# The sums T1 and T3 of a weight pair by an accumulating transfer, T2 and T4 on GpSimd one form earlier

## The chip, the cores and the metric

The kernel runs on one core of a Trainium2 chip. The metric is the device time of one execution, in microseconds; of several executions the median is compared. Five engines work side by side, each on its own list of instructions: TensorE (PE, with its weight loads PEld), VectorE (DVE), ScalarE (ACT), GpSimd (POOL) and SyncE (SP), which here only issues DMA transfers. Instructions wait for one another through semaphores.

## The reference

One layer of an encoder trunk on x of 512 positions by 1024 channels, in float32:

```python
h = _rmsnorm(x, g_pre_mix)
proj = h @ w_in                       # 1024 x 7168: q, k, v, g, u, sv, a_ret, a_sgu
...
y_ret = _retention_branch(q, k, v, g, ret_decay_logit, w_ret_o)
y_sgu = _sgu_branch(u, sv, sgu_ln_g, sgu_ln_b, w_spatial, b_spatial, w_sgu_o)
merged = jax.nn.sigmoid(a_ret) * y_ret + jax.nn.sigmoid(a_sgu) * y_sgu
x = x + _rmsnorm(merged @ w_out, g_post_mix)
h2 = _rmsnorm(x, g_pre_ffn)
x = x + _rmsnorm(_conv_gated_mlp(h2, w_up, conv_w, conv_b, w_down), g_post_ffn)
```

`w_up` is 1024 x 5632, `w_down` 2816 x 1024. The change concerns how the weights of `u`, of the two gates `a_ret` and `a_sgu`, and of most of `w_up` are brought in.

## The kernel before, in words

**Precision.** Each float32 operand is split into a high part (a copy to float32r on ACT, line 79) and a low part (source minus high part on DVE, line 86); `split` does both. A product is three matmuls: high by high, high by low, low by high.

**Pairs.** Two neighbouring weight blocks, each 128 x 1024 (four contraction tiles of 128 columns, two halves of S = 512), are multiplied in a Strassen-like scheme with seven products instead of eight. The weights come in seven forms: the blocks B11, B21 and B22 and the sums T1 = B11 + B12, T2 = T1 + B22, T3 = B12 + B22 and T4 = T2 + B21. Class `Pair` (line 676) multiplies them in the order B11, B21, T1, T2 (`part1`), T3 (`part2`), T4, B22 (`part3`); each product is twelve matmuls of 128x256. Between products ACT copies a result out of PSUM (`copy`, such as u<-ps, sig<-ps, c<-ps) or DVE adds it to another. There are twenty pairs:

- the U stage: four pairs, back to back, each with its `part3` behind the next one's `part1`;
- the gates: eight pairs in two halves of four (the first beside the retention's output block, the second beside the SGU's), with an ordinary block of 24 matmuls (`f_block`) after `part1` and one around `part3`;
- the couples: eight pairs of the up-projection, each with two `f_block`s as in the gates.

**Staging.** `wall` in device memory holds all weight blocks, in the order of use, arranged by the host; for pairs `_two` and `_up` lay out the blocks. A load is one 512 KB transfer issued from SP into a tile of the `raw` ring, which has four tiles (`raw_tile`, line 120); a tile is given to its next user when everything that reads it is done. Split blocks and forms go into the `w4` ring of nine slots (`slot`, line 126). `w_get` (line 203) hands out the next weight and emits the units behind it, up to nine slots ahead, so that loads, sums and splits stand in the engines' lists well ahead of the matmuls that use them. The Tile framework puts the instructions of each engine in an order and gives out buffers; SP issues all weight loads in the order of `wall`.

**A pair's forms before** (`w_form`, line 156): at the form B11 two loads bring `a` = [B11 | B12] and `b` = [B22 | B21] (lines 160 and 161). At T1 a third raw tile `t` is taken; DVE adds T1 into its first half (line 167) and T3 over B12 in `a` (line 168), and POOL adds T2 into the second half of `t` (line 169). At T4 POOL adds T4 over T2 (line 171). Each form is then split, the high part on ACT and the low part on DVE.

**Around the pairs.** POOL also issues the four xT loads ahead of the U stage (line 658, for the last two x tiles of each half, scaled by ACT on line 255) and adds the two gates' parts (line 806). Before the first pair, DVE multiplies the retention's output by its gate (L615), and PE transposes the result (L605 and L624, through `transposed` and `last_turn`).

Of the kernel before, what the change touches and what calls it, by code (L numbers as in the profile page):

```python
# [13 lines left out]
ALU = mybir.AluOpType  # L14
# [3 lines left out]
S = 512  # L18
# [29 lines left out]
def tile_block(ctx: ExitStack, tc, xT, x, wall, par, cs, wsp, bsp, gpost, gffn, out):  # L48
    nc = tc.nc
# [6 lines left out]
    def nm(s):  # L56
        uid[0] += 1
        return f"{s}_{uid[0]}"

    def blk(dt=F32, n="blk", shape=(P, S)):  # L60
        return sb.tile(list(shape), dt, tag="blk", bufs=NBLK, name=nm(n))

    def tmp(n="tmp", shape=(P, S)):
        return sb.tile(list(shape), F32, tag="tmp", bufs=6, name=nm(n))
# [19 lines left out]
    def split(hi, lo, src):  # L84
        copy(hi, src)
        nc.vector.tensor_sub(lo, src, as32(hi))  # L86
# [7 lines left out]
    i = 0  # L94
    while i < NW:
# [7 lines left out]
        elif i == UP0 + 2 * COUPLES[0][0]:  # L103
# [3 lines left out]
            i = UP0 + 2 * COUPLES[-1][1] + 2  # L107
# [10 lines left out]
    w_ready, w_pos, w_held, w_raw = {}, [0, 0], [0], {}  # L118

    def raw_tile():  # L120
        return sb.tile([P, 1024], F32, tag="raw", bufs=4, name=nm("raw"))
# [4 lines left out]
    def slot(n, at=0, w=1024):  # L126
        return sb.tile([P, 1088], F32R, tag="w4", bufs=9, name=nm(n))[:, at : at + w]
# [28 lines left out]
    def w_form(form, i):  # L156

        if form == "B11":
            a, b = raw_tile(), raw_tile()
            nc.sync.dma_start(a, wall[i])  # L160
            nc.sync.dma_start(b, wall[i + 1])
            w_raw["B11"], w_raw["B12"] = a[:, :S], a[:, S:]
            w_raw["B22"], w_raw["B21"] = b[:, :S], b[:, S:]
        elif form == "T1":
            t = raw_tile()
            w_raw["T1"], w_raw["T2"], w_raw["T3"], w_raw["T4"] = t[:, :S], t[:, S:], w_raw["B12"], t[:, S:]
            nc.vector.tensor_add(w_raw["T1"], w_raw["B11"], w_raw["B12"])  # L167
            nc.vector.tensor_add(w_raw["T3"], w_raw["B12"], w_raw["B22"])
            nc.gpsimd.tensor_tensor(out=w_raw["T2"], in0=w_raw["T1"], in1=w_raw["B22"], op=ALU.add)  # L169
        elif form == "T4":  # L170
            nc.gpsimd.tensor_tensor(out=w_raw["T4"], in0=w_raw["T2"], in1=w_raw["B21"], op=ALU.add)
        w = slot("wf", 0, 1088)
        lo, hi = w[:, AT_64 : AT_64 + S], w[:, S + AT_192 : 2 * S + AT_192]
        split(hi, lo, w_raw[form])
        return hi, lo
# [21 lines left out]
    def w_unit(u):  # L197
        return w_block(u[1]) if u[0] == "blk" else (w_down if u[0] in "qt" else w_form)(*u)
# [67 lines left out]
    for k in range(KD):  # L266
# [18 lines left out]
        for m in range(8):  # L285
            c = slice(m * P, (m + 1) * P)
# [5 lines left out]
    T0, T1 = slice(0, 256), slice(256, 512)  # L292
# [73 lines left out]
    for m in range(8):  # L366
        t = blk(n="qkraw")
# [286 lines left out]
    for n, acc in enumerate(t_group()):  # L654
        if n < 2:
            for k in (n + 2, n + 6):
                t = tmp("xT")
# [83 lines left out]
    for j in range(KD // 2):  # L741
        p = Pair(AF.Gelu_apprx_tanh, lambda: blk(n="u"), None, rbc)
# [52 lines left out]
    for j in range(KD // 2):  # L795
        for o, t in gated_pair(ogh, ogl, late if j == 0 else None):
            b = blk(n="r")
# [221 lines left out]
    i = 0  # L1019
    while i < NF:  # L1020
        if i in couples:
            p = Pair(None, lambda: tmp("c"), (h2h, h2l, h2forms))
# [179 lines left out]
def _parts(a, n, w):  # L1202

    k = a.shape[0] // P
    return a.reshape(k, P, n, w).transpose(2, 1, 0, 3).reshape(n, P, k * w)
# [15 lines left out]
def _two(a):  # L1221

    b = _parts(a, 8, P).reshape(4, 2, P, 2, S)
    return np.stack([
        np.concatenate([b[:, 0, :, 0], b[:, 1, :, 0]], -1), np.concatenate([b[:, 1, :, 1], b[:, 0, :, 1]], -1),
    ], 1)


def _up(a):

    for i, _ in COUPLES:
        b, c = a[2 * i].reshape(P, 2, S), a[2 * i + 1].reshape(P, 2, S)
        a[2 * i : 2 * i + 2] = np.stack([
            np.concatenate([b[:, 0], c[:, 0]], -1), np.concatenate([c[:, 1], b[:, 1]], -1),
        ])
    return a


def _gates(a, w):

    return np.concatenate([_two(a), _parts(w, 8, P).reshape(4, 2, P, 1024)], 1).reshape(16, P, 1024)
# [79 lines left out]
```

## Time and profile before

| | |
|---|---|
| device time, median of 3 runs | 825.94 us (825.88 to 827.58) |
| the profiled execution | 827.49 us, of which the profile's span is 825.7 us |
| granted TensorE clock | 0.999 of full speed |
| DVE additions for T1 and T3 | 40, 30.9 us together |
| POOL additions for T2 and T4 | 40, 62.9 us together |
| read from device memory | 88.19 MB |
| first pair's loads issued / last couple's T4 | 171.0 us / 657.6 us into the span |

In a row of the profile stand the start and the duration in us (or, in groups, the total busy time and the mean of one in ns), the engine, the line of the kernel, the operation, the tile written <- the tiles read, and the shape; behind an arrow in brackets stand the time the engine sat idle before it and what ended it. Rows "SPq" are transfers at the time SP issues them. L12 is line 12 of the kernel before. The windows' rows give, for a stretch of the span, the busy time and the number of instructions of PE, PEld, DVE, ACT and POOL, then the granted PE clock, the DMA engines' busy share and the GB/s that they moved.

### The profile page before, as it was taken

The numbers are of one execution on the slowest core, as the hardware profiler recorded it, in microseconds if no ns is written. First come the engines' busy times: TensorE is split into PE (matmuls) and PEld (weight loads), VectorE is DVE, ScalarE is ACT, GpSimd is POOL, SyncE is SP. The second block draws the span as 40 slices with busy tenths as digits, with TensorE's granted clock in tenths as the row PEclk, the third lists the DMA queues.
The fourth block names the chain that finished last, engine by engine and source line by source line (L and its number), as shares of the span: only waits on it lengthen the run. The fifth ranks groups of instructions, "written<-read, shape, count | busy, mean of one in ns | idle before, by whom it ended". The sixth has DMA issues, their size and how long they took to land.

```text
span 825.7 us, 13263 instructions
## 1 busy us (share of the span) xinstructions
PE 815.4 (99%) x5152; PEld 735.0 (89%) x5152; DVE 661.4 (80%) x1101; ACT 440.8 (53%) x771; POOL 101.0 (12%) x102
## 2 busy tenths in 40 slices
PE   9999999999999999999999999999999999999996
PEld 7888888888899999999988898899999998999996
DVE  7489897878797777767765568979899899988967
ACT  6636445546665444444445685556566566544531
POOL 0010000102121111132211211210111200000001
PEclk9999999999999999999999999999999999999999
DMA  8733222212223232222349111322322341233244
GB/s 294 246 116 102 77 77 77 77 52 78 90 102 129 103 102 80 101 101 103 108 166 339 48 55 55 103 102 103 102 103 102 102 154 52 77 115 129 96 147 154
DMA packets 29215, 93.24 MB, mean 113 GB/s; under 512 B 3360, under 2 KB 4000, under 8 KB 29152
## 3 DMA queue, kind: packets, MB, share of 16 engines
q1 hardware_dynamic: 26928, 86.85, 30.2%
q0 software_dynamic: 1360, 4.46, 1.6%
q10 hardware_dynamic: 864, 1.09, 0.4%
q8 instruction: 40, 0.66, 0.3%
q14 instruction: 23, 0.19, 0.1%
HBM read 88.19 MB, written 4.19 MB: 112 GB/s over the span
## 4 chain that ended last, share of the span: by engine, by line
PE 91%; DVE 6%; ACT 1%; issue 1%; DMA 0%; POOL 0%; DVEq 0%; SPq 0%; POOLq 0%; ACTq 0%
PE ps L692 23%; PE ps L217 12%; PE ps L218 12%; PE ps L219 12%; PE ps L1058 8%; PE ps L481 5%; PE ps L480 5%; PE ps L482 5%; PE ps L836 2%; PE ps L837 2%; PE ps L838 2%; PE ps L1074 1%; PE ps L761 1%; DVE fl L86 1%; PE ps L279 1%
## 5 line engine op out<-in xcount | busy, mean ns | idle before, releaser
L86 DVE TENSOR_TENSOR wl<-raw,wh 128x1024 fp32r<-128x1024 f32 (+1 forms) x93 | 109.1, 1182 | 48.9 <-PE ps L692 24.2
L79 ACT ACTIVATE wf<-raw 128x512 fp32r<-128x512 f32 x140 | 85.3, 627 | 102.7 <-PE ps L218 34.0
L86 DVE TENSOR_TENSOR wf<-raw,wf 128x512 fp32r<-128x512 f32 x140 | 111.1, 808 | 23.3 <-ACT wf L79 22.4
L692 PE MATMUL ps<-sh,wf 128*128 128x256 f32 x640 | 119.5, 277 | 0.0
L79 ACT ACTIVATE wh<-raw 128x1024 fp32r<-128x1024 f32 (+2 forms) x95 | 93.3, 993 | 37.4 <-DMA raw<-wall 17.0
L692 PEld LDWEIGHTS ps<-sh,wf 128*128 128x128 f32 x640 | 101.1, 188 | 0.8 <-ACT u L79 0.2
L217 PE MATMUL ps<-h2h,wh 128*128 128x512 f32 (+1 forms) x256 | 92.4, 363 | 0.7 <-ACT h2h L906 0.7
L218 PE MATMUL ps<-h2l,wh 128*128 128x512 f32 (+1 forms) x256 | 92.4, 363 | 0.0
L219 PE MATMUL ps<-h2h,wl 128*128 128x512 f32 (+1 forms) x256 | 92.1, 361 | 0.0
L692 PE MATMUL ps<-sl,wf 128*128 128x256 f32 x320 | 88.8, 278 | 0.0
L480 PE MATMUL ps<-wh,xh 128*128 128x512 f32 x192 | 75.0, 391 | 0.0
L481 PE MATMUL ps<-wl,xh 128*128 128x512 f32 x192 | 74.9, 390 | 0.0
L482 PE MATMUL ps<-wh,xl 128*128 128x512 f32 x192 | 74.8, 390 | 0.0
L169 POOL TENSOR_TENSOR raw<-raw,raw 128x512 f32<-128x512 f32 x20 | 36.2, 1809 | 235.2 <-DVE raw L167 207.8
L1058 PE MATMUL ps<-dl,fh 128*128 128x256 f32 x216 | 60.8, 281 | 0.1
L1058 PE MATMUL ps<-dh,fl 128*128 128x256 f32 x216 | 60.7, 281 | 0.0
L1058 PE MATMUL ps<-dh,fh 128*128 128x256 f32 x216 | 60.7, 281 | 0.0
L692 PEld LDWEIGHTS ps<-sl,wf 128*128 128x128 f32 x320 | 60.0, 188 | 0.6
L219 PEld LDWEIGHTS ps<-h2h,wl 128*128 128x128 f32 x256 | 48.0, 188 | 7.7
L217 PEld LDWEIGHTS ps<-h2h,wh 128*128 128x128 f32 x256 | 47.9, 188 | 7.9 <-ACT h2h L906 1.0
L692 PE MATMUL ps<-xh,wf 128*128 128x256 f32 x288 | 54.2, 278 | 0.0
L218 PEld LDWEIGHTS ps<-h2l,wh 128*128 128x128 f32 x256 | 48.0, 188 | 6.6
(314 smaller groups left out, 2048.9 us busy)
## 6 DMA issues: line engine op xcount, KB each, us to landing
raw<-wall SPq DMA_DIRECT2D x145, 512.0 KB, 3.6
x<-x SPq DMA_DIRECT2D x24, 256.0 KB, 5.9
xT<-xT SPq DMA_DIRECT2D x8, 256.0 KB, 5.4
x<-x POOLq DMA_DIRECT2D x8, 256.0 KB, 2.4
xT<-xT POOLq DMA_DIRECT2D x4, 256.0 KB, 3.6
out<-zg SPq DMA_DIRECT2D x4, 256.0 KB, 2.0
out<-zs ACTq DMA_DIRECT2D x3, 256.0 KB, 3.5
cs<-cs SPq DMA_DIRECT2D x2, 256.0 KB, 4.1
```

Source lines behind the costliest of these rows:

```text
L79: nc.scalar.activation(out=o, in_=i, func=AF.Copy)
L86: nc.vector.tensor_sub(lo, src, as32(hi))
L169: nc.gpsimd.tensor_tensor(out=w_raw["T2"], in0=w_raw["T1"], in1=w_raw["B22"], op=ALU.add)
L217: nc.tensor.matmul(o, ah, bh, start=start, stop=False)
L218: nc.tensor.matmul(o, ah, bl, start=False, stop=False)
L219: nc.tensor.matmul(o, al, bh, start=False, stop=stop)
L480: nc.tensor.matmul(acc[t], xh[k][:, c], wh[:, f], start=k == 0, stop=False)
L481: nc.tensor.matmul(acc[t], xh[k][:, c], wl[:, f], start=False, stop=False)
L482: nc.tensor.matmul(acc[t], xl[k][:, c], wh[:, f], start=False, stop=k == KD - 1)
L692: nc.tensor.matmul(o, w_[:, c], a_, start=first and k == n == 0, stop=k == 3 and n == 2, skip_group_check=True,)
L836: nc.tensor.matmul(o, ah, bh, start=k == 0, stop=False)
L1058: nc.tensor.matmul(o, a_[:, c], w_[:, f], start=j == t == i == 0, stop=j == DP - 1 and i == 2 and n not in (M2, M3, M4), skip_group_check= ...
```

## The change

```diff
     def w_form(form, i):
 
         if form == "B11":
-            a, b = raw_tile(), raw_tile()
+            t, a, b = raw_tile(), raw_tile(), raw_tile()
+            nc.sync.dma_start(t.rearrange("p (b c) -> p b c", b=2), wall[i : i + 2, :, :S].rearrange("b p c -> p b c"))
+            nc.gpsimd.dma_start(t, wall[i + 1], accum_op=ALU.add)
             nc.sync.dma_start(a, wall[i])
-            nc.sync.dma_start(b, wall[i + 1])
-            w_raw["B11"], w_raw["B12"] = a[:, :S], a[:, S:]
-            w_raw["B22"], w_raw["B21"] = b[:, :S], b[:, S:]
-        elif form == "T1":
-            t = raw_tile()
-            w_raw["T1"], w_raw["T2"], w_raw["T3"], w_raw["T4"] = t[:, :S], t[:, S:], w_raw["B12"], t[:, S:]
-            nc.vector.tensor_add(w_raw["T1"], w_raw["B11"], w_raw["B12"])
-            nc.vector.tensor_add(w_raw["T3"], w_raw["B12"], w_raw["B22"])
+            nc.sync.dma_start(b[:, :S], wall[i + 1, :, S:])
+            w_raw["T1"], w_raw["T3"] = t[:, :S], t[:, S:]
+            w_raw["B11"], w_raw["B21"] = a[:, :S], a[:, S:]
+            w_raw["B22"], w_raw["T2"], w_raw["T4"] = b[:, :S], b[:, S:], w_raw["B11"]
+        elif form == "B21":
             nc.gpsimd.tensor_tensor(out=w_raw["T2"], in0=w_raw["T1"], in1=w_raw["B22"], op=ALU.add)
-        elif form == "T4":
             nc.gpsimd.tensor_tensor(out=w_raw["T4"], in0=w_raw["T2"], in1=w_raw["B21"], op=ALU.add)
...
 def _two(a):
-        np.concatenate([b[:, 0, :, 0], b[:, 1, :, 0]], -1), np.concatenate([b[:, 1, :, 1], b[:, 0, :, 1]], -1),
+        np.concatenate([b[:, 0, :, 0], b[:, 0, :, 1]], -1), np.concatenate([b[:, 1, :, 0], b[:, 1, :, 1]], -1),
...
 def _up(a):
-            np.concatenate([b[:, 0], c[:, 0]], -1), np.concatenate([c[:, 1], b[:, 1]], -1),
+            np.concatenate([b[:, 0], b[:, 1]], -1), np.concatenate([c[:, 0], c[:, 1]], -1),
```

The host now stores a pair as [B11 | B21] and [B12 | B22]. A pair takes its three raw tiles at once. SP loads `t` with the first halves of both blocks, [B11 | B12], 512 KB in rows of 2 KB; a transfer issued from POOL adds the second block [B12 | B22] to it, so that `t` holds [T1 | T3]. SP loads `a` = [B11 | B21] whole and the half B22 into the first half of `b`. At the form B21 POOL adds T2 into the second half of `b` and T4 over B11 in `a`. A pair thus issues three transfers from SP (512, 512 and 256 KB) and one from POOL (512 KB read again); DVE's 40 additions are gone, and the splits, the products and PE's order are as before.

The tiles of the ring are given out in another order. In the gates from the second pair on, `t` takes the tile of the previous pair's `t`, `a` that of its `a` and `b` that of its `b`, so that they wait in turn for the splits of T3, of T4 and of B22 of the previous pair (the two blocks between use the fourth tile); the couples do the same. In the U stage `t` takes the tile of the `b` two pairs back, `a` that of the last pair's `t`, and `b` that of the last pair's `a`. The first pair's `b` takes the tile of an ordinary block loaded just before.

Where the order changes on SP, the start of the U stage (raw_1918 is the first pair's first tile; rows with 128x2x512 are `t`); before:

```order
L160 DMA raw_1918<-wall 128x1024
L161 DMA raw_1919<-wall 128x1024
L160 DMA raw_2062<-wall 128x1024
L161 DMA raw_2063<-wall 128x1024
L160 DMA raw_2249<-wall 128x1024
L161 DMA raw_2250<-wall 128x1024
```

and with the change:

```order
L160 DMA raw_1918<-wall 128x2x512
L162 DMA raw_1919<-wall 128x1024
L163 DMA raw_1920<-wall 128x512
L160 DMA raw_2062<-wall 128x2x512
L162 DMA raw_2063<-wall 128x1024
L163 DMA raw_2064<-wall 128x512
L160 DMA raw_2249<-wall 128x2x512
L162 DMA raw_2250<-wall 128x1024
L163 DMA raw_2251<-wall 128x512
```

Three loads stand where two stood, and `b` (L163) is the last of them.

On POOL, from just before the first pair (orstd belongs to the retention's norm, the xT rows are the loads of x for the U stage); before:

```order
L325 TENSOR_TENSOR orstd<-rs_1793,nhalf 128x4
L169 TENSOR_TENSOR raw_1973<-raw_1973,raw_1919 128x512
L658 DMA xT_1952<-xT 128x512
L658 DMA xT_1956<-xT 128x512
L658 DMA xT_2007<-xT 128x512
L658 DMA xT_2011<-xT 128x512
L171 TENSOR_TENSOR raw_1973<-raw_1973,raw_1919 128x512
L169 TENSOR_TENSOR raw_2176<-raw_2176,raw_2063 128x512
L739 DMA bst_2153<-bsp 128x512
L171 TENSOR_TENSOR raw_2176<-raw_2176,raw_2063 128x512
```

and with the change, where L168 makes T2, L169 makes T4 and L161 is the accumulating transfer:

```order
L161 DMA raw_1918<-wall 128x1024
L320 TENSOR_SCALAR rs_1793<-mv 128x4
L323 TENSOR_TENSOR orstd<-rs_1793,nhalf 128x4
L168 TENSOR_TENSOR raw_1920<-raw_1918,raw_1920 128x512
L656 DMA xT_1957<-xT 128x512
L656 DMA xT_1961<-xT 128x512
L656 DMA xT_2008<-xT 128x512
L169 TENSOR_TENSOR raw_1919<-raw_1920,raw_1919 128x512
L656 DMA xT_2012<-xT 128x512
L161 DMA raw_2062<-wall 128x1024
L168 TENSOR_TENSOR raw_2064<-raw_2062,raw_2064 128x512
L161 DMA raw_2249<-wall 128x1024
L169 TENSOR_TENSOR raw_2063<-raw_2064,raw_2063 128x512
```

The first pair's addition stands ahead of the norm's two small operations, its T4 ahead of the last xT load, and the third pair's addition (raw_2249) ahead of the second pair's T4 (raw_2063).

## The prediction

> **What bounds the kernel now.** I read the page first: the share of each engine, then the chain that ended last.
>
> ```profile
> PE 815.4 (99%) x5152; PEld 735.0 (89%) x5152; DVE 661.4 (80%) x1101; ACT 440.8 (53%) x771; POOL 101.0 (12%) x102
> PE 91%; DVE 6%; ACT 1%; issue 1%; DMA 0%; POOL 0%; DVEq 0%; SPq 0%; POOLq 0%; ACTq 0%
> ```
>
> TensorE (PE) is busy for 815.4 of 825.7 us and makes 91% of the chain. The change adds no matmul and takes none away, so it can gain only what PE waits for. Next the waits of PE:
>
> ```profile
> engine line waited for: us in total, times, longest us
> PE ps L264 <- DVE raw L259: 1.0, 1, 1.0
> PE ps L217 <- ACT h2h L906: 0.7, 1, 0.7
> PE ps L279 <- ACT wh L79: 0.4, 1, 0.4
> PE ps L624 <- DVE o L615: 0.3, 1, 0.3
> PE ps L605 <- DVE o L615: 0.3, 1, 0.3
> ```
>
> All named waits sum to 2.7 us. The first three lie outside the twenty pairs (the warm-up, the start of the FFN, the first weight block); the two on L615 are near pairs, 0.6 us together. Last the stretches that hold the pairs (U stage, gates, up-projection):
>
> ```profile
> core 0: us, PE busy (x) PEld busy (x) DVE busy (x) ACT busy (x) POOL busy (x), PEclk, DMA share, GB/s
> 216.00:263.00 47.00, 46.98 (x392) 46.60 (x393) 42.87 (x64) 30.00 (x55) 11.72 (x8) 1.00 0.30 103
> 263.00:426.00 163.00, 163.00 (x1061) 147.98 (x1060) 117.07 (x183) 72.92 (x122) 29.50 (x19) 1.00 0.32 110
> 505.00:702.00 197.00, 197.00 (x1202) 175.58 (x1201) 177.84 (x275) 117.11 (x197) 25.61 (x16) 1.00 0.29 100
> ```
>
> PE is busy for 46.98 of 47, 163 of 163 and 197 of 197 us. VectorE (DVE) is nearly full beside it (42.87 of 47, 177.84 of 197), but it keeps up. So the change is worth what it spoils, plus some tenths of a us.
>
> **What goes from DVE.**
>
> ```profile
> L168 DVE TENSOR_TENSOR raw<-raw,raw 128x512 f32<-128x512 f32 x20 | 17.1, 853 | 1.0 <-DMA raw<-wall 0.7
> L167 DVE TENSOR_TENSOR raw<-raw 128x512 f32<-128x512 f32 x20 | 13.8, 688 | 1.5 <-DMA raw<-wall 1.4
> L169 POOL TENSOR_TENSOR raw<-raw,raw 128x512 f32<-128x512 f32 x20 | 36.2, 1809 | 235.2 <-DVE raw L167 207.8 <-DMA raw<-wall 27.4
> ```
>
> The forty additions for T1 and T3 go: 13.8 + 17.1 = 30.9 us of DVE. All of it lies beside a busy PE, so it shortens the end only where PE waits for DVE. At 215.9 us one such pair stands ahead of the last L615, but that product then waits for ScalarE (ACT), and I take **−0.1** there (bounds −0.3, the whole wait on L624, and 0). T2 and T4 stay on GpSimd (POOL) with their durations.
>
> **What comes: loads, and X.** A pair now moves 512 KB into `t`, 512 KB again for the addition, 512 KB into `a` and 256 KB into `b`: 1.75 MB for 1 MB, at 16 engines used to 0.29 to 0.32 in these stretches. 1.75 times that is under 0.6, so the mean rate has room, and what counts is the time until T1 and T3 are usable. Call X the time from `t` landed to the addition landed. No accumulating transfer is in the trace.
>
> ```profile
> raw<-wall SPq DMA_DIRECT2D x145, 512.0 KB, 3.6
> xT<-xT POOLq DMA_DIRECT2D x4, 256.0 KB, 3.6
> x<-x POOLq DMA_DIRECT2D x8, 256.0 KB, 2.4
> ```
>
> One plain 512 KB load takes 3.6 us (median) from issue to landing. A transfer that reads source and destination and writes can cost one such pass (X = 3.6, the low end) to three (10.8, the high end). It can't be below the one pass, since it moves these bytes. I take **5.5**, between one pass and two, since part of a load's 3.6 us is fixed (a 256 KB one from the GpSimd queue takes 2.4). The Trainium skill, page "Collectives: The Full Stack", section "The bandwidth ceiling: the fold count and why AG ≠ RS ≠ AR", says that an add within a transfer is slower than a copy because it needs two source reads, not because of the addition; by it X is nearer to two passes (an estimate of 7.2), and the sum below would be 1.7 us higher, by the second couple. No run here shows it yet.
>
> How late may T1 be? In the gates of the first half:
>
> ```profile
> 321.37 0.33 SPq L160 DMA_DIRECT2D raw<-wall  x1
> DMA to landing us min/median/max: 4.4/4.4/4.4
> 334.66 1.15 ACT L79 ACTIVATE wf<-raw 128x512 fp32r<-128x512 f32 x2 [4.33 <-PE ps L218]
> 336.25 0.39 ACT L79 ACTIVATE sig<-ps 128x256 f32<-128x256 f32 x1 [0.44 <-PE ps L692]
> 338.80 0.28 PE L692 MATMUL ps<-xh,wf 128*128 128x256 f32 x1
> 365.97 0.33 SPq L160 DMA_DIRECT2D raw<-wall  x1
> 381.60 0.28 PE L692 MATMUL ps<-xh,wf 128*128 128x256 f32 x1
> 560.47 0.33 SPq L160 DMA_DIRECT2D raw<-wall  x1
> 576.42 0.28 PE L692 MATMUL ps<-h2h,wf 128*128 128x256 f32 x1
> ```
>
> The load that starts a pair is issued at 321.37 and lands 4.4 later, at 325.8 (the row on landing is that line's in this stretch). ACT makes T1's and T2's high parts at 334.66; the evacuation at 336.25 stands behind them in ACT's queue, and the product at 338.80 overwrites what it reads. With the change T2 (1.8 on POOL, L169's mean) follows the addition, then T2's copy (0.6), then the evacuation (0.39): 325.8 + X + 1.8 + 0.6 + 0.39 ≤ 338.8 gives **X ≤ 10.2**. A pair of the second four gates (365.97, 381.60), with the same 4.4, bears **X ≤ 8.4**, a couple (560.47, 576.42, with the median landing of 3.6) **X ≤ 9.6**. At 5.5 these sixteen pairs wait for nothing, but for the second couple below: 0 us. That couple apart, what hides X is the early load, a dozen us ahead of its use.
>
> **First pair.** Its `b` takes the ring slot that the weight block split at 184.22 gives up.
>
> ```profile
> 184.22 1.22 DVE L86 TENSOR_TENSOR wl<-raw,wh 128x1024 fp32r<-128x1024 f32 x1 [0.91 <-PE ps L481]
> 186.30 1.74 POOL L169 TENSOR_TENSOR raw<-raw,raw 128x512 f32<-128x512 f32 x1 [4.41 <-DVE raw L167]
> 189.59 0.69 DVE L615 TENSOR_TENSOR o<-o,g 128x512 f32<-128x512 f32 x1 [0.39 <-ACT g L614]
> 226.64 1.78 POOL L169 TENSOR_TENSOR raw<-raw,raw 128x512 f32<-128x512 f32 x1 [4.19 <-DMA raw<-wall]
> 227.19 1.78 DVE L86 TENSOR_TENSOR wf<-raw,wf 128x512 fp32r<-128x512 f32 x1
> ```
>
> The slot is free at 185.44; 2.9 us later (256 KB: between 2.4 and 3.6) `b` is there, and T2 runs from about 188.4 to 190.1 instead of 186.3 to 188.0. The row at 227.19 shows what a DVE operation beside a POOL addition costs: 1.78 instead of 0.69. Now the L615 at 189.59, for which PE waits, meets T2: it ends at 190.1 + 0.69 = 190.8 instead of 190.28. **+0.5** (bounds 0 if they miss each other, +1.1 for the whole 1.78 − 0.69). Queued behind T2 on POOL are the four xT transfers, two us later and one of them behind T4; their ACT readers come after 194.8 and feed forms that PE reads in the U stage: 0, else under 1 us.
>
> **U stage.** T2 now waits for a load that waits for T4's split of the pair before.
>
> ```profile
> 210.52 0.33 SPq L160 DMA_DIRECT2D raw<-wall  x1
> 221.07 1.39 POOL L171 TENSOR_TENSOR raw<-raw,raw 128x512 f32<-128x512 f32 x1 [7.75 <-DVE wf L86]
> 223.04 0.33 SPq L161 DMA_DIRECT2D raw<-wall  x1
> 223.22 0.69 DVE L86 TENSOR_TENSOR wf<-raw,wf 128x512 fp32r<-128x512 f32 x1 [0.20 <-ACT wf L79]
> ```
>
> Before, the load that T2 needs left at 223.04 and T2 ran at 226.64. Now it leaves after the split that ends at 223.91, and being half as long lands at about 226.8: T2 is 0.2 to 0.6 later, three times, and ACT's evacuations have about as much room. On POOL the third pair's addition stands ahead of the second pair's T4 and waits for its `t`, but that leaves at 210.5 and lands by 215, six us before T4's 221.07. **+0.2** (bounds −0.3 and +1.0).
>
> **First couple to second.**
>
> ```profile
> 514.38 0.63 ACT L79 ACTIVATE wf<-raw 128x512 fp32r<-128x512 f32 x1 [2.92 <-POOL raw L169]
> 523.66 0.33 SPq L160 DMA_DIRECT2D raw<-wall  x1
> 534.78 0.37 ACT L79 ACTIVATE c<-ps 128x256 f32<-128x256 f32 x1
> ```
>
> ACT's 2.92 us wait for T2 in the first couple goes (its additions are done long before), but PE did not wait for it. The second couple's `t` leaves at 523.66, or about 0.7 earlier as DVE is freer, lands 4.5 later at 527.5 (three loads together; two took 4.4), the addition at 533.0, T2 at 534.8, its copy and the evacuation at 535.8, against 535.15 before: **+0.6** (at X = 3.6 nothing; at 7.2 +2.3).
>
> **Sum**: −0.1 + 0 + 0.5 + 0.2 + 0.6 = **+1.2 us**. The profiled execution took 827.49 us (span 825.7 and 1.8 around it), 1.55 above the median of 825.94; with the change such a one would have a span of 826.9. On the median: **827.1 us**. The bounds together give −0.6 to +4.4.
>
> **The rivals.**
> 1. *The addition is slow.* From X = 8.4 the second gates stall on every pair, from 9.6 the couples, from 10.2 the first gates. At the high end of 10.8 that costs 4 × 2.4 + 6 × 1.2 + 4 × 0.6 = 19.2 us, and the second couple 5.9: 25.1 with these, 0.6 for the rest, about 851.6. At X = 9.4 it is 4 × 1.0 + 4.5 + 0.6, about 835. For it: X is in no row. Against it: it takes nearly three passes. The Trainium skill, page "SBUF — State Buffer", section "SBUF: two separate sides", speaks for it: descriptors of a transfer issued from GpSimd can't be written while a DVE operation holds the port that both share; that could add one such DVE operation (1.78) to X. The traced transfers from that queue, 3.6 and 2.4 us beside a working DVE, show little of it.
> 2. *The relief pays.* PE's 0.6 us on L615 goes, and in the U stage PE issues faster:
>
> ```profile
> 223.00:250.00 27.00, 27.00 (x229) 27.00 (x229) 1.00 0.33 117
> ```
>
> That is 27.00 / 229 = 118 ns a matmul; in the gates the 24 from 338.80 to 341.52 take 113. If a freer DVE brought that back, 392 × 5 ns = 1.9 us, together about 823.5. Against it: PE's weight loads are back to back there (27.00 of 27), and no DVE row stands between.
> 3. *T1 and T3 were never in the way, and nothing is late*: the losses above are hidden by queued weights, and the time is 825.9.
>
> **How the numbers follow.** A measurement of this kernel tells about 0.2%, 1.65 us, from no change: "same" is 824.3 to 827.6. My forecast 0.58 (of that 0.20 above 827.6, by the upper bounds of the four terms), rival 1 0.15, rival 2 0.12, rival 3 0.15. So faster 0.12, same 0.38 + 0.15 = 0.53, slower 0.35. The range goes from 824.3 (half of rival 2 is below) to 834, which takes in the upper bounds and X up to 9.3.
>
> **What would show it.** Right: no L167 or L168 on DVE and its total near 630 us; the addition landing 5 to 6 us after issue; T2 at 188 us and PE's wait on L615 near 190 us longer; a wait of some tenths at the second couple; no wait in the gates. Wrong: waits of PE behind the evacuations once in each gate or couple (rival 1), or a U stage under 46 us (rival 2). The forecast fails first in X, then in which loads share the engines.

## The result, and the profile after

The changed kernel took 830.85 us (median of 5, 829.42 to 832.94), the kernel before 825.94; the ratio is 1.0064, with a 95% interval of 1.0035 to 1.0094. It is slower by some 5 us, where 1.2 were forecast. The profiled execution took 832.94 us with a span of 831.2, 5.5 us more than before's 825.7.

The page of the kernel after: busy time, chain, and the transfers from the two queues (KB each, median us to landing).

```profile
PE 817.7 (98%) x5152; PEld 735.3 (88%) x5152; DVE 635.5 (76%) x1061; ACT 437.9 (53%) x771; POOL 127.1 (15%) x122
PE 77%; DVE 9%; DMA 6%; ACT 3%; POOL 2%; issue 2%; POOLq 0%; DVEq 0%; ACTq 0%; SPq 0%
raw<-wall SPq DMA_DIRECT2D x145, 512.0 KB, 4.0
raw<-wall POOLq DMA_DIRECT2D x20, 512.0 KB, 5.7
```

DVE is spared 25.9 us (661.4 to 635.5) and PE does the same work. But the chain that ends last has gone from 91% PE to 77%: DVE has 9% of it, transfers 6%, ACT 3% and POOL 2%. The addition lands 5.7 us after its issue (the forecast took 5.5); the plain loads beside it slowed from 3.6 to 4.0. The waits of PE at the pairs and just ahead of them, after:

```profile
PE ps L690 <- ACT sig L79: 1.9, 2, 1.5
PE ps L690 <- ACT c L79: 0.9, 1, 0.9
PE ps L603 <- DVE o L613: 0.6, 1, 0.6
PE ps L690 <- ACT u L79: 0.4, 1, 0.4
PE ps L622 <- DVE o L613: 0.3, 1, 0.3
```

Three are new, on L690 (the products of a pair, L692 before): behind ACT's evacuations sig, c and u. The wait on L603 (L605 before) went from 0.3 to 0.6. The windows say where, with a finer cut than before's: U stage, first gate pair, the other gates, first two couples, the rest.

```profile
216.00:263.00 47.00, 45.91 (x384) 45.00 (x383) 37.84 (x57) 28.59 (x55) 13.03 (x11) 1.00 0.55 149
263.00:282.00 19.00, 17.51 (x103) 15.08 (x102) 10.60 (x17) 8.24 (x13) 3.78 (x3) 1.00 0.48 124
282.00:426.00 144.00, 144.00 (x944) 130.96 (x943) 100.32 (x152) 64.09 (x110) 30.79 (x24) 1.00 0.51 145
505.00:545.00 40.00, 39.05 (x213) 33.52 (x212) 32.70 (x48) 20.34 (x35) 14.12 (x5) 1.00 0.37 104
545.00:702.00 157.00, 156.90 (x982) 140.34 (x981) 132.12 (x208) 94.31 (x160) 29.63 (x18) 1.00 0.48 136
```

PE is idle for 1.1 us of the U stage, 1.5 at the first gate pair and 1.0 at the first couples, and for nothing in the other seven gate pairs. The busy share of the DMA engines in the U stage went from 0.30 to 0.55.

PE's order is the same in both kernels, so the start of the same matmul can be set against itself. By this count the 5.4 us between the two executions (from PE's first matmul) are: 0.3 in the warm-up, no part of the change; 0.3 at the first pair; 0.9 in the U stage; 2.0 at the first gate pair; 0 from there to the FFN; 1.2 at the second couple; 0.7 in later couples. A wait counts a little more here than in the table of waits (2.0 for 1.5), since PE's next matmuls are slower too. These are the sizes in one execution. In two others with the same edit at this place, those of e5b_nblk74 and e6_c0_dve below, the first gate pair lost 1.0 and 1.1 us and the U stage 1.5 and 1.6.

**The first gate pair.** SP's issues, POOL, ACT and PE there, after:

```profile
259.18 0.38 SPq L160 DMA_DIRECT2D raw<-wall  x1
260.12 0.33 SPq L162 DMA_DIRECT2D raw<-wall  x1
261.52 0.33 SPq L163 DMA_DIRECT2D raw<-wall  x1
263.48 0.33 SPq L133 DMA_DIRECT2D raw<-wall  x1
264.15 0.90 POOL L161 DMA_DIRECT2D raw<-wall  x1 [10.14 <-DVE u L727]
DMA to landing us min/median/max: 8.5/8.5/8.5
272.79 0.63 ACT L79 ACTIVATE wf<-raw 128x512 fp32r<-128x512 f32 x1 [4.74 <-DMA raw<-wall]
274.17 0.63 ACT L79 ACTIVATE wf<-raw 128x512 fp32r<-128x512 f32 x1 [0.75 <-POOL raw L168]
274.71 0.37 ACT L79 ACTIVATE sig<-ps 128x256 f32<-128x256 f32 x1
275.13 0.39 PE L690 MATMUL ps<-xh,wf 128*128 128x256 f32 x1 [1.49 <-ACT sig L79]
```

The wait can be followed back here. The load at 259.18 is the `t` of the sixth pair, the second of the gates: it and its addition are made ahead, while PE is still in the first. The addition, issued at 264.15, ran beside the loads issued from 260.12 to 263.48 and took 8.5 us instead of 5.7 (the row on landing is that of this one transfer). T1's split on ACT waited 4.74 us for it. T2 followed on POOL and its split waited 0.75 more. Behind that split, in ACT's queue, stood the first pair's evacuation sig at 274.71, whose product PE had finished at 270.9, and PE waited for it until 275.13, to go on with the first pair.

**The second couple.** POOL, ACT, SP and PE:

```profile
507.67 9.04 POOL L168 TENSOR_TENSOR raw<-raw,raw 128x512 f32<-128x512 f32 x1 [6.08 <-DMA raw<-wall]
516.74 0.63 ACT L79 ACTIVATE wf<-raw 128x512 fp32r<-128x512 f32 x1 [5.88 <-POOL raw L168]
526.40 0.38 SPq L160 DMA_DIRECT2D raw<-wall  x1
531.52 0.90 POOL L161 DMA_DIRECT2D raw<-wall  x1 [13.44 <-DVE c L707]
537.46 1.29 POOL L168 TENSOR_TENSOR raw<-raw,raw 128x512 f32<-128x512 f32 x1 [5.04 <-DMA raw<-wall]
539.74 0.39 PE L690 MATMUL ps<-h2h,wf 128*128 128x256 f32 x1 [0.95 <-ACT c L79]
```

T2 of the first couple, 1.3 us in the median of the pairs, took 9.04 us on POOL: from 507.67 on DVE ran without a gap until 515.6, and T2 ended 1.1 us later. ACT waited 5.88 us for it, the splits of T2 and T3 came late, and with them the issue of the second couple's `t` (526.40; the first load stood at 523.66 before). The addition then left no earlier than 531.52. PE's wait at 539.74 lies in the first couple again, behind the evacuation c, which stood behind the second couple's T2.

### The profile page after: what moved, and what is told of

Its sections match the earlier page's. It is cut to its first block, busy times and chain, and to the rows that moved or that the text cites. A ratio compares the mean times of both kernels' runs of the same rounds, so it can differ in the third digit from the quotient of the medians.

```text
span 831.2 us, 13360 instructions
## 1 busy us (share of the span) xinstructions
PE 817.7 (98%) x5152; PEld 735.3 (88%) x5152; DVE 635.5 (76%) x1061; ACT 437.9 (53%) x771; POOL 127.1 (15%) x122
## 4 chain that ended last, share of the span: by engine, by line
PE 77%; DVE 9%; DMA 6%; ACT 3%; POOL 2%; issue 2%; POOLq 0%; DVEq 0%; ACTq 0%; SPq 0%
PE ps L690 16%; PE ps L215 10%; PE ps L216 10%; PE ps L217 9%; PE ps L1056 8%; DMA raw<-wall 6%; PE ps L478 5%; PE ps L479 5%; PE ps L480 5%; POOL raw L168 2%; DVE wf L86 2%; PE ps L836 2%; PE ps L834 2%; PE ps L835 2%; PE ps L1072 1%
## 5 line engine op out<-in xcount | busy, mean ns | idle before, releaser
L86 DVE TENSOR_TENSOR wf<-raw,wf 128x512 fp32r<-128x512 f32 x140 | 114.9, 833 | 61.8 <-ACT wf L79 60.2
L86 DVE TENSOR_TENSOR wl<-raw,wh 128x1024 fp32r<-128x1024 f32 (+1 forms) x93 | 106.3, 1152 | 40.8 <-issue 18.4
L690 PE MATMUL ps<-sh,wf 128*128 128x256 f32 x640 | 120.1, 278 | 0.8 <-ACT u L79 0.4
L690 PEld LDWEIGHTS ps<-sh,wf 128*128 128x128 f32 x640 | 101.2, 188 | 2.3 <-ACT u L79 0.8
L690 PE MATMUL ps<-sl,wf 128*128 128x256 f32 x320 | 88.8, 277 | 0.0
L168 POOL TENSOR_TENSOR raw<-raw,raw 128x512 f32<-128x512 f32 x20 | 43.1, 2155 | 134.3 <-DMA raw<-wall 112.4
L690 PEld LDWEIGHTS ps<-sl,wf 128*128 128x128 f32 x320 | 60.0, 188 | 0.6
L690 PE MATMUL ps<-xh,wf 128*128 128x256 f32 x288 | 54.2, 279 | 1.5 <-ACT sig L79 1.5
```

What stands on the lines that cost most here:

```text
L690: nc.tensor.matmul(o, w_[:, c], a_, start=first and k == n == 0, stop=k == 3 and n == 2, skip_group_check=True,)
```

## The experiments

Theory A: the loss is a sum of separate waits; the long time of the addition makes those at the first gate pair and the second couple, the turn of the ring, with three tiles taken at once, that of the U stage. The rivals (the ring alone, the queue and the shared engines, DVE's part) are told with each run.

Each was measured beside the kernel before, whose median was 824.56, 824.46 and 825.96 us in the three batches (of 29, 11 and 21 runs; e1 to e4, e5 to e7, and e8 and e9), so a ratio is good to some 0.2% across batches; within a batch they compare better.

**e1_dve_sums**: the additions back on DVE, in the change's tiles.

```diff
-            nc.gpsimd.dma_start(t, wall[i + 1], accum_op=ALU.add)
...
-            nc.sync.dma_start(b[:, :S], wall[i + 1, :, S:])
+            nc.sync.dma_start(b, wall[i + 1])
...
         elif form == "B21":
+            nc.vector.tensor_add(w_raw["T1"], w_raw["T1"], w_raw["B12"])
+            nc.vector.tensor_add(w_raw["T3"], w_raw["T3"], w_raw["B22"])
```

> The accumulating transfer undone: b is loaded whole ([B12|B22], 512 KB), DVE adds it to t at the form B21; the three tiles, their turn in the ring and the places of T2 and T4 stay as in the change. Theory A (the losses at the first gate pair and the second couple come from the time that the addition in the transfer takes, those in the U stage from taking three tiles of the ring at once): the waits of 1.6 us at 275 us and 1.1 us at 540 us go, those of 0.6 us at 254 and 260 us stay; 827.0 to 828.5 us. Rival R (all of it is the ring's turn, whoever makes T1 and T3): all four waits stay, 830 to 831 us. Rival D (what DVE is spared already pays, and comes back as a loss here): over 831 us.

Measured: 837.88 us, ratio 1.0159 (1.0137 to 1.0181). Beyond every expectation but D's, and not for D's reason:

```profile
PE ps L691 <- ACT c L79: 3.2, 3, 1.1
PE ps L691 <- ACT u L79: 2.5, 1, 2.5
PE ps L623 <- DVE o L614: 2.0, 1, 2.0
```

```profile
L167 DVE TENSOR_TENSOR raw<-raw,raw x20: 683/692/695, 189.1 to 662.9; 128x512 f32<-128x512 f32 x20
its engine sat idle before it (us, times) until:
  DMA raw<-wall: 3.7, 9
who waited for it (us, times):
...
  ACT wf L79: 8.4, 6
```

Behind the waits of PE stand the rows on L167, the sum T1: DVE sat idle for 3.7 us in nine of them because of a load, and ACT for 8.4 us because of T1. That load is `b`, last of the three to get a tile; T1 on DVE needs it, T1 by the transfer doesn't. The long wait of 2.5 us costs more than itself, since the granted clock fell after it:

```profile
249.00:251.00 2.00, 2.00 (x12) 2.00 (x11) 1.97 (x4) 1.49 (x3) 0.00 (x0) 0.50 0.27 45
```

The clock (the third number from the end) was 0.50 here, a matmul came every 0.21 us instead of every 0.12, and set matmul against matmul the place lost 4.1 us. So the run is no clean undoing: it shows that this turn of the ring is bad for sums on DVE, not what the transfer costs. The next two runs price that.

**e2_plain** and **e3_none**: the second transfer without the addition, and no second transfer.

```diff
-            nc.gpsimd.dma_start(t, wall[i + 1], accum_op=ALU.add)
+            nc.gpsimd.dma_start(t, wall[i + 1])
```

> The second transfer of a pair is a plain load from the POOL queue to the same place, without the addition, so T1 and T3 hold B12 and B22 in place of the sums: that part of the computation is changed. It prices the addition apart from the queue and the bytes. Theory A (the time X is that of an addition, two reads): its landing falls from 5.7 us to some 4 us, the wait at the first gate pair from 1.6 to under 0.5 us, and the time is 828 to 829.5 us. Rival Q (X is the POOL queue and the shared engines, the addition costs nothing): the landing stays above 5.3 us and the time within 1 us of the change, 830 to 832 us.

> The second transfer is left out, so T1 and T3 are B11 and B12: that part of the computation is missing. DVE is spared its 40 additions and nothing takes their place; the ring is as in the change. It bounds what sparing DVE can bring, and shows what the ring alone costs. Theory A: no wait at the first gate pair or the second couple, the U stage's waits of 0.6 us stay: 826.5 to 828 us. Rival R (the ring alone): 829.5 to 831 us. Rival P (the sparing of DVE pays once the transfer's wait is gone): under 824.5 us.

Measured: e2_plain 825.80 us, ratio 1.0025 (1.0012 to 1.0039); e3_none 825.27 us, ratio 1.0010 (0.9999 to 1.0022). The page of e2_plain, and its wait on L603 (it has none on L690 long enough for the table):

```profile
raw<-wall POOLq DMA_DIRECT2D x20, 512.0 KB, 4.6
```

```profile
PE ps L603 <- DVE o L613: 0.6, 1, 0.6
```

The plain transfer lands in 4.6 us, the addition in 5.7, and with the 1.1 us go the waits at the first gate pair and the second couple (by its ratio the result is at the lower edge of theory A's band, 828 us to 825.94). So of the change's 0.64%, the addition makes about 0.4%, the second reading some 0.15% and what is left, the ring and the place of T2, 0.1%. The first has an uncertainty of some 0.3%, since it comes from two batches, the others of 0.1 to 0.2%. Rival Q falls, and R too. One half of theory A falls with them: it had the U stage's waits stay in e3_none, with the same turn of the ring, but neither run has a wait at a U pair's product that is long enough for the table. So the ring's turn alone doesn't make those waits; the additions are needed for them. P falls as well: in e3_none DVE is spared its sums, and nothing is paid for them, and still it is not faster. Matmul by matmul its profiled execution won 1.2 us in the first half of the U stage and had lost 0.9 of it again by the end, most of that in the same stage. What it won there is no wait but a faster pace of PE, which comes with DVE's sums too (last section).

**e4_mixed**: the transfer in thirteen pairs only.

```diff
+        if GATE0 + 4 <= i < GATE1 or i >= UP0 + 2 * COUPLES[2][0]:
             ...
+        else:
             ...
```

> The accumulating transfer in thirteen of twenty pairs: the gates from the second pair on and the couples from the third on. The U stage, the first gate pair and the first two couples make their sums as before the change (DVE T1 and T3, three tiles in two steps). Theory A (the loss sits in those seven pairs' transitions, the thirteen others cost nothing and gain nothing): 825.3 to 827 us, no wait over 0.4 us in the gates or couples. Rival S (each accumulating pair costs a little, by shared DMA engines or POOL): 13/20 of the loss stays, 828.5 to 829.5 us. Rival P (the sparing of DVE pays where nothing waits): under 824.5 us.

Measured: 826.61 us, ratio 1.0026 (1.0015 to 1.0037), between A and S. The waits on L706 (the pairs' products here), and the split ahead of the second:

```profile
PE ps L706 <- ACT u L79: 1.2, 1, 1.2
PE ps L706 <- ACT sig L79: 0.5, 1, 0.5
272.78 0.63 ACT L79 ACTIVATE wf<-raw 128x512 fp32r<-128x512 f32 x1 [0.66 <-POOL raw L169]
```

The first wait, at 249 us, lies ahead of all pairs that have the transfer, in a U pair whose sums DVE makes and whose tiles now turn in another order. The second, at 274 us, is the one of the changed kernel: L169 is here T2 of the second gate pair, the first to have the transfer, whose addition took 9.3 us. Matmul by matmul the execution is 2.3 us behind from there to the FFN and 2.5 to 2.8 in the couples. So the six steady gate pairs cost nothing (S falls there) and gain nothing, and the couples cost half a microsecond together. That the first wait belongs to the passage from one kind of pair to the other is likely, but no run shows it.

**e5_ring5**, **e5b_nblk74** and **e9_before_ring5**: five raw tiles, and two controls.

```diff
-NBLK = 76
+NBLK = 74
...
-        return sb.tile([P, 1024], F32, tag="raw", bufs=4, name=nm("raw"))
+        return sb.tile([P, 1024], F32, tag="raw", bufs=5, name=nm("raw"))
```

The first is the change with both lines, e5b_nblk74 the change with the first alone, e9_before_ring5 the kernel before with both.

> The change with five tiles in the raw ring instead of four, and 74 instead of 76 tiles in the ring of general blocks to make room. Theory A (the transfer with addition takes 5.7 us, and what makes it late is that the ring gives t its tile only when T3 of the pair before is split): t and a leave one tile earlier, the waits at the first gate pair, the second couple and the U stage go; ratio to the kernel before 1.000 to 1.002. Rival C (the engines are shared by more loads, and an earlier issue only makes more of them run together): two of the four waits stay, 1.004 to 1.007.

> The control for five tiles: the change with 74 instead of 76 general blocks and four raw tiles. If the blocks do not matter, the ratio is that of the change, 1.005 to 1.008; if they do, it is higher, and the run with five tiles is to be read against this one.

> The kernel before with five raw tiles and 74 general blocks, to read the change with five tiles against. There the U stage ran 2 us ahead of the kernel before and lost 2.3 us at 441 us, where the output projection waits for weights. Theory G (the gain and the wait belong to five tiles, whoever makes the sums): ratio 0.998 to 1.001 with the same wait near 441 us. Rival T (they belong to the transfer, which spares DVE): no gain in the U stage, no wait at 441 us, 1.000 to 1.002.

Measured: e5_ring5 828.32 us, 1.0053 (1.0041 to 1.0065); e5b_nblk74 831.05, 1.0082 (1.0064 to 1.0100); e9_before_ring5 828.74, 1.0031 (1.0020 to 1.0042). The waits of e5_ring5, then those of e9_before_ring5:

```profile
PE ps L835 <- DVE wl L86: 0.9, 1, 0.9
PE ps L834 <- ACT wh L79: 0.6, 1, 0.6
```

```profile
PE ps L837 <- DVE wl L86: 0.9, 1, 0.9
PE ps L836 <- ACT wh L79: 0.7, 1, 0.7
```

The control e5b_nblk74 is at 1.0082, the change at 1.0064 in another batch: the intervals overlap, so the two blocks fewer aren't shown to cost anything. With five tiles no wait on L690 is left: the transfer is issued a tile earlier, and although it lands later (7.7 us in the median, with more loads at once) nothing waits for it. That half of theory A holds, and rival C's waits don't come. The ratio is C's all the same, by a wait for the output projection's weights, 2.1 us matmul by matmul at 441 us. It comes in the kernel before with five tiles too, as theory G had it, with 1.0 more at 433; so e9_before_ring5 is slower than either expectation. Up to there e5_ring5 had won 2.1 us and e9_before_ring5 1.4: 0.3 at the first pair in both, the rest in the U stage. The kernel before has no wait in the U stage to win back (PE busy for 46.98 of 47 us), so that rest is the faster pace of PE told in the last section and not the fifth tile's by any wait.

**e6_c0_dve**: T2 of the first couple on DVE.

```diff
+            t2 = nc.vector if i == UP0 + 2 * COUPLES[0][0] else nc.gpsimd
-            nc.gpsimd.tensor_tensor(out=w_raw["T2"], in0=w_raw["T1"], in1=w_raw["B22"], op=ALU.add)
+            t2.tensor_tensor(out=w_raw["T2"], in0=w_raw["T1"], in1=w_raw["B22"], op=ALU.add)
```

> T2 of the first couple alone is added on DVE instead of POOL, where it took 9.0 us beside a full DVE. Theory A (that addition held up T2's split, hence T3's and the issue of the second couple's t, and so made the wait of 1.1 us at 540 us): ACT's wait of 5.9 us at 517 goes, t leaves 1.5 to 3 us earlier, the wait at 540 us goes, and the ratio is 1.004 to 1.006 (1.2 us below the change). Rival X (that wait is the transfer's own 5.7 us): it stays, ratio 1.006 to 1.008.

Measured: 827.67 us, ratio 1.0044 (1.0032 to 1.0056). SP and POOL in e6_c0_dve:

```profile
523.41 0.38 SPq L160 DMA_DIRECT2D raw<-wall  x1
528.64 0.89 POOL L161 DMA_DIRECT2D raw<-wall  x1 [9.51 <-DVE gp L970]
534.62 1.29 POOL L169 TENSOR_TENSOR raw<-raw,raw 128x512 f32<-128x512 f32 x1 [5.09 <-DMA raw<-wall]
```

`t` leaves at 523.41 instead of 526.40 (0.6 of it because this execution was that much ahead by then), the addition at 528.64, T2 runs at 534.62, and the wait on L691 behind c is gone; the transfer's own time there is unchanged (5.8). Rival X falls: one POOL addition, starved for 9 us, was the cause, and it ended 23 us ahead of PE's wait.

**e7_halves**: T1's half first; **e8_halves_c0**: the same with e6_c0_dve's edit.

```diff
-            nc.gpsimd.dma_start(t, wall[i + 1], accum_op=ALU.add)
+            nc.gpsimd.dma_start(t[:, :S], wall[i + 1, :, :S], accum_op=ALU.add)
+            nc.gpsimd.dma_start(t[:, S:], wall[i + 1, :, S:], accum_op=ALU.add)
```

> The second transfer in two halves of 256 KB, T1's first. Theory A (T1 is late by the transfer's time, which for half the bytes is some 1.3 us shorter): the first gate pair's wait of 1.6 us falls to about 0.5, the second couple's to 0; ratio 1.002 to 1.005. Rival F (the time is mostly fixed for each transfer, or the two halves queue): T1 is ready no earlier, one more issue of 0.9 us on POOL makes T2 later, ratio 1.006 to 1.010.

> Both remedies on the change: the second transfer in two halves, T1's first, and T2 of the first couple on DVE. Theory A (the loss is a sum of separate waits, each with its own cause): the first gate pair and the second couple wait for nothing, the U stage and the first pair keep their 1 to 2.5 us; ratio 1.002 to 1.005. Rival W (the waits are not separate: what one gives back the next takes): 1.005 to 1.008, with a wait elsewhere in the couples.

Measured: e7_halves 828.96 us, 1.0061 (1.0044 to 1.0077); e8_halves_c0 828.34, 1.0030 (1.0018 to 1.0041). In e7_halves the row on landing of the first half, over all pairs, and PE's wait at the pairs:

```profile
DMA to landing us min/median/max: 3.9/4.6/6.7
```

```profile
PE ps L691 <- ACT u L79: 2.0, 2, 1.7
```

T1 is ready a microsecond earlier (4.6 for 5.7), and the waits at the first gate pair and the second couple are gone, as A expects. But the U stage now loses 3.1 us matmul by matmul (3.5 in e8_halves_c0) where the whole transfer lost 0.9 to 1.6: there are four transfers and four POOL issues more in it, beside the loads of `a` and `b`. Which of these does it was not separated. So e7_halves has A's mechanism (T1 earlier, two waits gone) and F's ratio; e8_halves_c0 has A's ratio and its two waits gone, but its U stage lost more than A's 1 to 2.5 us. No version here is faster than the kernel before.

## Why the prediction was right, and where its sum was too small

The time lies in the forecast range, and the mechanism is the forecast one: nothing to gain, and a loss by late additions. But the loss of 4.9 us is four times the +1.2 of the sum, and above even the terms' upper bounds together (+4.4). The range took the time in only by the room that it left for a larger X, so the hit owes more to a wide range than to the sum. "Same", which had the larger chance (0.53), did not come; slower had 0.35. The terms one by one:

- *What bounds the kernel: held.* DVE lost 25.9 us of work and PE's time did not follow. e3_none, with DVE's sums gone for nothing, is 0.1% slower than before, not faster; rival 2's gain didn't come.
- *X, 5.5 us: too small.* From its issue to its landing the addition took 5.7 us in the median, but X was to count from `t`'s landing, and POOL's issue comes half a microsecond or more behind that: so counted X was 6.4 in the median of the twenty pairs. *The assumption that it is one number failed:* it was 5.9 to 9.0 us (5.4 to 8.5 from the issue), longest beside several loads.
- *"These sixteen pairs wait for nothing, but for the second couple: 0 us": failed at one place,* and the sign "no wait in the gates" with it. PE lost nothing in seven gate pairs, as reckoned. In the first it lost 2.0 us, the largest term of all, by the addition of the second. This place's limit was not reckoned: the sum used those of two later ones (10.2 and 8.4). The rows of the kernel before would have given it:

```profile
255.92 0.33 SPq L160 DMA_DIRECT2D raw<-wall  x1
271.90 0.28 PE L692 MATMUL ps<-xh,wf 128*128 128x256 f32 x1
```

  By the prediction's own working (4.4 to land, 2.79 behind X) that is X ≤ 8.8. With the change `t` left at 259.18, 3.3 us later, while PE was only 1.6 behind, so 1.7 less. From `t`'s landing (259.18 and about 4.4) to the addition's (264.15 and 8.5) it took 9.0 us, and PE waited 1.5; the limit was thus near 7.5. Rival 1 had this mechanism, put to the second half's gates and to X over 8.4 everywhere; it came about at one place.
- *Second couple, +0.6 (to 2.3): 1.2.* Right place, right end of the range, but for a reason that the working missed: it set T2 of the first couple down as "done long before", while the row it quoted, with ACT's 2.92 us wait for a POOL addition, already showed that POOL starves beside this DVE stretch. With the change it starved for 9.0 us, and e6_c0_dve shows that this set `t`'s issue.
- *U stage, +0.2 (to 1.0): 0.9* (1.5 and 1.6 in the two other executions). T2's start in the third and fourth pair followed `b`, as said, but `b` and `a` were later than "half as long a load" allows: the fourth pair's `a` landed only 5.4 us after its issue, beside the addition and the load of `b`, while the term took the quiet time of a load. Without the addition, in e3_none, that load took 4.5 us, and no wait of the table was left in this stage.
- *First pair, +0.5: 0.3.* The collision came, smaller. *L624, −0.1: 0*; the wait is 0.3 as before.
- *Later couples, 0: 0.7*, half of it at the fourth, where T2 took 3.9 us on POOL.

The rule quoted from the Trainium skill ("Collectives: The Full Stack", "The bandwidth ceiling: the fold count and why AG ≠ RS ≠ AR"), that an add in a transfer costs by its second read, has the right sign here: 5.7 us with the addition, 4.6 without. But two full passes (7.2) are too many: the price is 1.1 us for 512 KB. The Trainium skill's page "SBUF — State Buffer" ("SBUF: two separate sides") says that of a GpSimd operation and a DVE one at the shared port the first to start has it for its whole length and the other waits. The 9.04 us of L168 agree as to the waiting, but not as to the order: its row starts while DVE's operations come and go, and all of them went ahead of it (unless the row begins before POOL had the port, which the trace doesn't tell).

## What to carry to other kernels

Work taken from an engine that is 80% busy is worth nothing where another is at 99%, and its replacement must be priced at its worst place, not at a steady one: what counted here was the addition that left right behind four loads in 4.3 us. A replacement by a transfer trades a steady time (0.69 us for T1 on DVE) for one that depends on what else is in flight (5.4 to 8.5 us here). And a wait is best followed back beyond its releaser: at the second couple the cause ended 23 us earlier, on another engine.

## What the runs showed of the hardware

An addition within a 512 KB transfer from the POOL queue cost 1.1 us over a plain one, and 0.88 us of POOL for its issue instead of 0.56.

A POOL addition of 1.3 us took 9.0 us beside a DVE without gaps, and 3.9 to 4.3 us in three later couples.

PE has two paces for 128x256 matmuls in the last stage, on the same code with no waits. For 750 to 800 us, the kernel before, then e4_mixed:

```profile
750.00:800.00 50.00, 50.00 (x427) 50.00 (x426) 1.00 0.36 126
750.00:800.00 50.00, 50.00 (x443) 50.00 (x443) 1.00 0.39 121
```

427 matmuls against 443, 117 ns against 113 each, at the same granted clock. The faster pace set in after a wait of 0.3 us at the start of the stage in the profiled executions of e1_dve_sums, e4_mixed, e5b_nblk74, e6_c0_dve and e8_halves_c0. The kernels before and after, e2_plain, e3_none and e7_halves had that wait too and stayed slow; the two with five tiles had none and stayed slow. Over the stage the pace makes 3.1 us, some two thirds of the spread of the kernel before (822.7 to 827.6 us) and of what the change costs. It differs between executions of the same code, so it is likely a part of the noise in the ratios above; the runs without a profile don't show it.

The U stage has the same two paces. The kernel before ran at 118 ns there (229 matmuls in 27 us, shown in the prediction). For 223 to 250 us, e5_ring5, then e9_before_ring5:

```profile
223.00:250.00 27.00, 27.00 (x240) 27.00 (x239) 1.00 0.68 186
223.00:250.00 27.00, 26.81 (x233) 26.42 (x233) 1.00 0.34 109
```

The first is 113 ns throughout; the second has it between short waits, with all sums on DVE. So this is the pace that rival 2 spoke of, but it is not DVE's relief that brings it. What sets it was not tried in either stage.
